# Two query-latent blocks as a column pair, closer last attention steps, alternating output blocks, and a fourth seven-product quad in the last pair

## The chip, the cores and the metric

The kernel runs on one core of a Trainium2 chip. Five engines share the work: TensorE (PE, matrix products and transposes), VectorE (DVE), ScalarE (ACT), GpSimd (POOL) and SyncE (SP, which only issues DMAs here). The metric is the time of one execution on the device in microseconds (us).

## The reference

The reference is a two-layer decoder trunk on x of 256 rows by 2048 columns, all in fp32. Layer 0 is retention with 8 heads and an MLP; layer 1 is multi-head latent attention with 16 heads and an MLP. Cut to the parts that the change touches:

```python
def mla_attention(h, w_dq, q_norm, w_uq, ...):        # layer 1
    c_q = rms_norm(h @ w_dq, q_norm)                  # 2048 -> 1536, the query latent
    q = (c_q @ w_uq).reshape(b, s, H, 128 + 64)       # 16 heads
    ...                                               # norms, rope, causal softmax over k_nope, k_pe
    return o @ w_o                                    # 2048 -> 2048

def sq_relu_mlp(h, w1, w2):                           # 2048 -> 8192 -> 2048
    return jnp.square(jax.nn.relu(h @ w1)) @ w2

x = x + mla_attention(rms_norm(x, norm_mix[1]), ...)
x = x + sq_relu_mlp(rms_norm(x, norm_mlp[1]), w1, w2)
```

## The kernel before, in words

**Products in fp32.** TensorE gets every fp32 operand as a high and a low part. ACT makes the high part by a cast (L185, or L188 with a scale), VectorE the low part by subtracting it from the source (L186, or L189). One product is then three matmuls: high by high, high by low, low by high. Activations (`act_tile`, 24 buffers) hold both parts of two 128-wide slices of the contraction for all 256 rows.

**Weights** come in chunks of up to 1 MB on SP's queue into `raw` (4 buffers) and are split half by half into tiles `wh` and `wl` of 128 x 1024 (5 buffers each). TensorE reads them in the same order, so a low-part tile that VectorE makes late holds TensorE up, and VectorE can be ahead by no more than five tiles.

**Plain products.** `gemm` computes a block of 512 columns (or fewer) over all chunks: 24 matmuls for one chunk of 512 columns.

**Column pairs.** `gemm_pair` (L335) computes two blocks of 512 columns together. Each chunk (a `quad`, L282) is a 2 x 2 block product: two row tiles of 128 by two slices of the contraction, times two slices by two column blocks. It takes either eight products (24 matmuls) or, after Strassen and Winograd, seven (21 matmuls). A seven needs sums of the weights, made by three VectorE additions (L321, L324, L325), four low-part tiles in place of two, and sums of the activations, which `with_sums` (L392 to L400) makes on VectorE with one more split. The tuples `THREE`, `FOUR` and `HEAD` list which quads of eight are sevens. `pair_out` (L367) copies six accumulators out of PSUM on ACT and finishes the combination with four VectorE additions; then every block is the sum of two parts, which are added later into x or by `summed` (L389).

**The order of the work.** Python code walks through the weight chunks. `later(n, fn)` puts a step n chunks ahead, `tick` runs the steps that have come due after each chunk, and `need` runs steps early until a wanted activation exists. A scheduler then fixes each engine's order of instructions at build time; on the chip every engine executes in that order.

**PSUM.** Four banks `acc` hold accumulators. Two banks `tp` take turns for transposes, attention outputs and two of the pair's products. A two-bank tile `at` holds the scores or the pair's last two products.

**Layer 1.** `into_next` adds the last MLP result into x, transposes and splits it twice, for the kv projection (`act_kv`) and for the query latent (`act_q`). The kv projection `kd` has two blocks; `downed` (L860) evacuates them and queues the transposes `kpe_tp` and `ckvtp` two chunks later. The query latent `dq` is three `gemm` blocks of four chunks (L934), each evacuated by `queried` (L912). Eight chunks `ku` make keys and values. Then `uq` makes the queries of two heads at a time, b = 0 to 7, three chunks each; `query` (L978) queues a turn three chunks later that transposes (`qntp`, `qptp`), that queues `score` (L1018) three later, that queues the transposes `ptp` three later, and those `values` (L1068) two later, which leaves the attention output `ao` in a `tp` bank until ACT and VectorE have split it into `ot`. The output projection `wo` (`gemm_blocks`, L418) starts with blocks 0 and 1, three chunks of block 0 and then three of block 1, and then the last chunk of each, which needs the last heads. The MLP of layer 1 has four groups of hidden columns; the last group ends with the pair `d_30` (columns 0 to 1023, eight quads), called the last pair here, and the plain blocks `d_32` and `d_33`. `finish` (L1086) adds each block into x and writes it out.

Of the kernel before, what the change touches and what calls it, by code (L numbers as in the profile page):

```python
# [15 lines left out]
AF = mybir.ActivationFunctionType  # L16
ALU = mybir.AluOpType
# [3 lines left out]
P = 128  # L21
NT = 2
# [18 lines left out]
S = NT * P  # L41
D = 2048
KD = D // P
NB = 4
# [2 lines left out]
NOPE, ROPE, MV, KVR, QR = 128, 64, 128, 512, 1536  # L47
KV_NBS, Q_NB = (320, 256), 384
GROUPS = (4, 4, 4, 4)
THREE, FOUR, HEAD = (3, 5, 7), (1, 3, 5, 7), (2, 4, 6, 7)  # L50
PI = math.pi

G_MIX0, G_MLP0, G_KV, G_MIX1, G_MLP1 = 0, 16, 32, 48, 64
# [15 lines left out]
def yoco(ctx: ExitStack, tc: tile.TileContext, a):  # L69
# [29 lines left out]
    def later(n, fn):  # L99
        queue.append((clock[0] + n, next(count), fn))  # L100
# [317 lines left out]
    def gemm_blocks(w, chunk_of, act, nk, name, done):  # L418

        n = nk // 4  # L420
        first = [accs(512, f"{name}{b}") for b in range(2)]
        for b in range(2):
            for g in range(n - 1):
                piece(w, chunk_of(b) + g, first[b], act, g, nk, 512, f"{name}{b}")
        for b in range(2):
            last_piece(w, chunk_of(b), first[b], act, nk, 512, f"{name}{b}", lambda acc, b=b: done(b, acc))
        for b in range(2, NB):
            gemm(w, chunk_of(b), act, nk, 512, f"{name}{b}", lambda acc, b=b: done(b, acc))

    def x_block_t(blocks, b, g0s, outs, name, sums):  # L430

        for k2 in range(2):
            tp = transposed(
                lambda t, j: blocks[t][:, (2 * k2 + j) * P : (2 * k2 + j + 1) * P], f"{name}_tp{b}{k2}"
            )
            for g0, out in zip(g0s, outs):
                scales = [gain(g0 + b * 4 + k2 * 2 + j) for j in range(2)]
                v = act_tile(f"{name}{g0}_{b}{k2}")
                if not sums:
                    split_act(v, tp, scales)  # L440
                    out.append(v)
                elif 2 * b + k2 in FOUR:
                    u = f2k([2, S], f"{name}u_{b}{k2}")
                    for j in range(2):
                        nc.scalar.activation(u[:, j], tp[:, j], AF.Copy, scale=scales[j])
                    split_act(v, u)
                    out.append((v, with_sums(u, f"{name}{b}{k2}")))
                else:
                    split_act(v, tp, scales)
                    out.append((v, None))  # L450
# [13 lines left out]
            if ss is not None:  # L464
                square_sum(x[t][b], ss[t][:, b : b + 1], f"{name}_{t}{b}")

    def into_next(ss, g0s, outs, r, name, sums=False):


        def done(b, acc):  # L470
            add_to_x(acc, b, ss, name)
            blocks = [x[t][b] for t in range(NT)]
            for t in range(NT):
                nc.gpsimd.dma_start(x_home[t][b], blocks[t])
            later(1, lambda: x_block_t(blocks, b, g0s, outs, name, sums))
            if b == NB - 1:
                r.extend(x_rstd(ss, name))

        return done
# [223 lines left out]

    ss = [small(NB, f"ss1_{t}") for t in range(NT)]
    act, r = [], []
    into_n1 = into_next(ss, [G_MLP0], [act], r, "n1", True)
    halves = [[], []]

    def ret_projected(h, qk, gate, v, s):
# [74 lines left out]
    def mlp(layer, act, r, done):  # L784
        w1, w2 = a[f"mlp_w1_{layer}"], a[f"mlp_w2_{layer}"]
        f0 = 0
        for gi, nf in enumerate(GROUPS):
            hid, blocks = [], []
            last = gi == len(GROUPS) - 1

            def up(c, p, hid=hid, blocks=blocks, last=last):

                need(r, NT)
                c = summed(c)
                for t in range(NT):
                    for i in range(2):
                        nc.scalar.activation(c[t][i], c[t][i], AF.Relu, scale=r[t])

                def turn(i):
                    for q in (2 * i, 2 * i + 1):  # L800
                        name = f"hid{layer}_{p}{q}"
                        tp = transposed(
                            lambda t, j: c[t][q // 2][:, (q % 2 * 2 + j) * P : (q % 2 * 2 + j + 1) * P], f"{name}_tp"
                        )
                        u = f2k([2, S], f"{name}_u")
                        nc.scalar.activation(u, tp, AF.Square)
                        v = act_tile(name)
                        split_act(v, u)
                        blocks.append((v, with_sums(u, name) if len(blocks) in (THREE if last else FOUR) else None))
                        hid.append(v)  # L810

                later(0, lambda: turn(0))
                later(1, lambda: turn(1))

            for p in range(f0 // 2, (f0 + nf) // 2):
                kinds = THREE[not (p or layer) :] if p % 2 or not p else FOUR
                gemm_pair(
                    w1, p * 8, act, [i in kinds for i in range(8)], f"u{layer}_{p}", lambda c, p=p, up=up: up(c, p)
                )
            if last:  # L820
                x_tiles(f"mlp{layer}")
            for p in range(2):
                if last and p and layer:
                    for b in (2, 3):
                        need(hid, 2 * nf)
                        gemm(
                            a["mlp_w2t"], (b - 2) * nf, hid, 4 * nf, 512, f"d{layer}_{gi}{b}",
                            lambda acc, b=b: done(b, acc),
                        )
                    continue  # L830

                def add(c, p=p, last=last):
                    into_x(done, c, p) if last else to_home(c, p)

                kinds = [i in (FOUR if p and not last else THREE) for i in range(2 * nf)]
                gemm_pair(w2, p * 32 + 2 * f0, blocks, kinds, f"d{layer}_{gi}{p}", add)
            f0 += nf

    ss = [small(NB, f"ss2_{t}") for t in range(NT)]
    act_kv, act_q, r2 = [], [], []  # L840
    mlp(0, act, r, into_next(ss, [G_KV, G_MIX1], [act_kv, act_q], r2, "n2"))


    def pe_rope(dst, u, src, t, i, heads):
# [15 lines left out]
    def downed(acc, b):  # L860
# [33 lines left out]
                split_act(v, tp, [gain(G_CKV + 2 * k2 + j) for j in range(2)])  # L894
                ckv.append(v)

        later(2, turn)

    first = [accs(n, f"kd{b}") for b, n in enumerate(KV_NBS)]
    for rows in (range(2), range(2, 4)):  # L900
# [8 lines left out]
    ssq = [small(3, f"ssq{t}") for t in range(NT)]  # L909
    cq, rq = [], []  # L910

    def queried(acc, b):  # L912
        cqb = []
        for t in range(NT):
            c = f2k([512], f"cq{b}{t}")
            nc.scalar.activation(c, acc[t], AF.Copy, scale=r2[t])
            square_sum(c, ssq[t][:, b : b + 1], f"cq{b}{t}")
            cqb.append(c)
            if b == 2:
                tot = small(1, f"cqtot{t}")  # L920
                nc.vector.reduce_sum(tot, ssq[t], axis=AX.X)
                rq.append(rstd(tot, QR, 1, f"cq{t}"))

        def turn():
            for k2 in range(2):
                tp = transposed(lambda t, j: cqb[t][:, (2 * k2 + j) * P : (2 * k2 + j + 1) * P], f"cqtp{b}{k2}")
                v = act_tile(f"cq{b}{k2}")
                split_act(v, tp, [gain(G_CQ + b * 4 + 2 * k2 + j) for j in range(2)])
                cq.append(v)

        later(1, turn)

    for b in range(3):
        gemm(a["mla_w_dq"], b * 4, act_q, KD, 512, f"dq{b}", lambda acc, b=b: queried(acc, b))  # L934


    k_t, v_s, vs = [], [], []
# [38 lines left out]
    def query(acc, b):  # L976
# [28 lines left out]
        def turn():  # L1005
            tp = transposed(lambda t, j: qr[t][0][:, j, 0:NOPE], f"qntp{b}")
            raw = f2k([2, S], f"qt{b}")
            nc.scalar.activation(raw, tp, AF.Copy, scale=gqn)
            qt = [f2k([2, S], f"qt{b}{i}", F32R) for i in range(2)]
            split(qt[0], qt[1], raw)  # L1010
            tp = transposed(lambda t, j: qr[t][1][:, j].rearrange("p i c -> p (i c)"), f"qptp{b}")
            qpe = f2k([2, S], f"qpe{b}", F32R)
            nc.scalar.copy(qpe, tp)
            later(3, lambda: score(b, qt, qpe))

        later(3, turn)

    def score(b, qt, qpe):  # L1018

# [36 lines left out]
        def turn():  # L1056
            pt = []
            for hh in range(2):
# [3 lines left out]
                o = f2k([3 * P], f"pt{b}{hh}")  # L1062
                nc.scalar.copy(o, tp)
                pt.append(o)
            later(2, lambda: values(b, pt))

        later(3, turn)

    def values(b, pt):
        o = bank("tp", [2, S], f"ao{b}")  # L1070
        for hh in range(2):
            nc.tensor.matmul(o[:, hh], v_s[b][:, 0, hh], pt[hh][:, 0:S], start=True, stop=False)
            nc.tensor.matmul(o[:, hh, P:S], v_s[b][:, 1, hh], pt[hh][:, S:], start=False, stop=True)
        v = act_tile(f"ot{b}")
        split_act(v, o)
        o_act.append(v)

    for b in range(8):
# [2 lines left out]
    ss = [small(NB, f"ss3_{t}") for t in range(NT)]  # L1081
    act, r = [], []
    x_tiles("wo")
    gemm_blocks(a["mla_w_o"], lambda b: b * 4, o_act, KD, "wo", into_next(ss, [G_MLP1], [act], r, "n3", True))

    def finish(b, acc):  # L1086
        add_to_x(acc, b, None, "")
        for t in range(NT):
            nc.sync.dma_start(a["out"][t * P : (t + 1) * P, b * 512 : (b + 1) * 512], x[t][b])

    mlp(1, act, r, finish)
    while queue:
# [93 lines left out]
```

## Time and profile before

| what | value |
|---|---|
| median of 3 runs | 2477.12 us (2475.17 to 2477.81) |
| profiled execution | 2474.51 us |
| its span | 2472.7 us |
| granted TensorE clock | 1.00 |
| ACT busy in the span | 1606.1 us (65%) |
| HBM read | 479.14 MB |

The span runs from the first to the last instruction of the program; the execution's time holds 1.8 us around it. A row of the waits gives the waiting engine, line and tile, the engine, tile and line that it waited for, and then the sum in us, how often, and the longest. A row of the windows gives length, and for each engine the busy time and the number of instructions. A row of the timeline gives start and length in us from the start of the span, engine, line, operation, output and inputs. A tile's name ends with a stage or block: `d_wl` is a low-part tile of an MLP's second matrix, `dq_wl` one of the query latent.

### The profile page before, as it was taken

What the parts mean: (1) busy time and instruction counts of PE and PEld (TensorE: products, weight loads), DVE (VectorE), ACT (ScalarE), POOL (GpSimd) and SP (SyncE); (2) the same over time, 40 slices, a digit from 0 to 9 for tenths busy, and PEclk for the clock granted to TensorE, in tenths of its full rate; (3) what the DMA queues carried; (4) which work ended last, traced back from release to release, by engine and by line L of the source; (5) the groups of instructions that cost most, each with busy time, mean ns of one, the idle gap of its engine ahead of it and who ended that gap; (6) DMA issues with size and microseconds to landing.
All of it is one profiled execution on the core that took longest, in us unless ns stands there. A gap on an engine that the chain in (4) does not pass through costs nothing.

```text
span 2472.7 us, 31711 instructions
## 1 busy us (share of the span) xinstructions
PE 2455.6 (99%) x11635; PEld 2060.0 (83%) x11635; DVE 2167.4 (88%) x2805; ACT 1606.1 (65%) x2253; POOL 251.6 (10%) x310
## 2 busy tenths in 40 slices
PE   9999999999999999999999999999999999999999
PEld 7888888888888888888888888998888888888887
DVE  7799899889899999999999967776689999999996
ACT  6566656556676667667666766676566666676663
POOL 7300011000010010110110101110000201101100
PEclk9999999999999999999999999999999999999999
DMA  9555567555564685684785564445545856857854
GB/s 328 211 174 205 196 205 234 199 192 201 198 236 182 209 262 216 213 254 172 246 263 196 192 228 168 153 155 179 199 174 199 261 212 209 268 203 225 266 192 153
DMA packets 93403, 521.04 MB, mean 211 GB/s; under 512 B 11072, under 2 KB 12224, under 8 KB 40000
## 3 DMA queue, kind: packets, MB, share of 16 engines
q1 hardware_dynamic: 71856, 472.83, 53.8%
q0 software_dynamic: 21248, 46.15, 8.5%
q8 instruction: 91, 1.49, 0.2%
q14 instruction: 64, 0.52, 0.1%
q10 hardware_dynamic: 144, 0.05, 0.0%
HBM read 479.14 MB, written 39.85 MB: 210 GB/s over the span
## 4 chain that ended last, share of the span: by engine, by line
PE 91%; DVE 4%; ACT 3%; issue 1%; POOL 1%; DMA 0%; SPq 0%; ACTq 0%; POOLq 0%; DVEq 0%
PE u_c L358 7%; PE u_c L356 7%; PE u_c L357 7%; PE d_c L357 6%; PE d_c L358 6%; PE d_c L356 6%; PE rk_acc L274 2%; PE rq_acc L274 2%; PE rp_c L356 2%; PE rp_c L357 2%; PE rp_c L358 2%; PE u_p L358 2%; PE u_p L356 2%; PE u_p L357 2%; PE d_p L356 2%; PE d_p L358 2%
## 5 line engine op out<-in xcount | busy, mean ns | idle before, releaser
L185 ACT CAST u_wh<-u_raw 128x1024 fp32r<-128x1024 f32 x362 | 347.9, 991 | 207.8 <-DVE u_raw L321 100.8
L185 ACT CAST d_wh<-d_raw 128x1024 fp32r<-128x1024 f32 x358 | 344.1, 993 | 202.5 <-DVE d_raw L321 93.9
L186 DVE TENSOR_TENSOR u_wl<-u_raw,u_wh 128x1024 fp32r<-128x1024 f32 x362 | 402.0, 1144 | 47.2 <-ACT u_wh L185 41.7
L186 DVE TENSOR_TENSOR d_wl<-d_raw,d_wh 128x1024 fp32r<-128x1024 f32 x358 | 397.8, 1146 | 40.1 <-ACT d_wh L185 35.5
L356 PE MATMUL u_c<-u_wh,n 128*128 128x512 f32 x706 | 276.4, 392 | 0.0
L357 PE MATMUL u_c<-u_wl,n 128*128 128x512 f32 x706 | 275.5, 390 | 0.0
L358 PE MATMUL u_c<-u_wh,n 128*128 128x512 f32 x706 | 274.9, 389 | 0.0
L356 PE MATMUL d_c<-d_wh,hid 128*128 128x512 f32 x654 | 256.0, 392 | 0.0
L357 PE MATMUL d_c<-d_wl,hid 128*128 128x512 f32 x654 | 255.4, 391 | 0.0
L358 PE MATMUL d_c<-d_wh,hid 128*128 128x512 f32 x654 | 254.6, 389 | 0.0
L185 ACT CAST rp_wh<-rp_raw 128x1024 fp32r<-128x1024 f32 (+1 forms) x166 | 160.7, 982 | 140.9 <-DVE rp_raw L321 64.9
L186 DVE TENSOR_TENSOR rp_wl<-rp_raw,rp_wh 128x1024 fp32r<-128x1024 f32 (+1 forms) x166 | 184.9, 1137 | 26.7 <-ACT rp_wh L185 24.4
L358 PEld LDWEIGHTS u_c<-u_wh,n 128*128 128x128 f32 x706 | 132.6, 188 | 27.4
L356 PEld LDWEIGHTS u_c<-u_wh,n 128*128 128x128 f32 x706 | 132.6, 188 | 26.9
L357 PEld LDWEIGHTS u_c<-u_wl,n 128*128 128x128 f32 x706 | 132.6, 188 | 26.7
L358 PEld LDWEIGHTS d_c<-d_wh,hid 128*128 128x128 f32 x654 | 122.8, 188 | 25.4
L356 PEld LDWEIGHTS d_c<-d_wh,hid 128*128 128x128 f32 x654 | 122.8, 188 | 25.2
L357 PEld LDWEIGHTS d_c<-d_wl,hid 128*128 128x128 f32 x654 | 122.9, 188 | 24.7
L150 POOL DMA_DIRECT2D xh<-d_c x48 | 41.6, 867 | 856.6 <-ACT d_c L373 854.7
L185 ACT CAST ro_wh<-ro_raw 128x1024 fp32r<-128x1024 f32 x88 | 85.7, 997 | 59.7 <-DVE ro_raw L321 25.7
L356 PE MATMUL rp_c<-rp_wh,a 128*128 128x512 f32 x286 | 111.9, 391 | 0.0
L357 PE MATMUL rp_c<-rp_wl,a 128*128 128x512 f32 x286 | 111.4, 390 | 0.2 <-DVE rp_wl L186 0.2
(465 smaller groups left out, 6075.6 us busy)
## 6 DMA issues: line engine op xcount, KB each, us to landing
u_raw<-in_mlp_w SPq DMA_DIRECT2D x128, 1024.0 KB, 5.2
d_raw<-in_mlp_w SPq DMA_DIRECT2D x120, 1024.0 KB, 4.9
rp_raw<-in_ret_w_gv SPq DMA_DIRECT2D x56, 1024.0 KB, 4.9
ro_raw<-in_ret_w_out SPq DMA_DIRECT2D x32, 1024.0 KB, 4.9
uq_raw<-in_mla_w_uq SPq DMA_DIRECT2D x24, 768.0 KB, 4.1
rq_raw<-in_ret_w_qk SPq DMA_DIRECT2D x16, 1024.0 KB, 5.0
rk_raw<-in_ret_w_qk SPq DMA_DIRECT2D x16, 1024.0 KB, 4.8
wo_raw<-in_mla_w_o SPq DMA_DIRECT2D x16, 1024.0 KB, 4.8
```

The costliest lines, as they stand in the source:

```text
L150: nc.gpsimd.dma_start(x_home[t][2 * p + j], part, accum_op=ALU.add)
L185: nc.scalar.copy(h, src)
L186: nc.vector.tensor_tensor(l, src, h.bitcast(F32), op=ALU.subtract)
L274: nc.tensor.matmul(acc[f], wh[:, cols], a.rearrange("p i s -> p (i s)"), start=k == 0, stop=k == nk - 1)
L356: nc.tensor.matmul(dst, ah, bh, start=n == 0, stop=False)
L357: nc.tensor.matmul(dst, ah, bl, start=False, stop=False)
L358: nc.tensor.matmul(dst, al, bh, start=False, stop=n == total[key] - 1)
```

## The change

1. The first two of the three dq blocks become a `gemm_pair` whose quads 4 to 7 are sevens (`QUERY`); the third stays a `gemm`. The activations of those four quads are copied scaled to SBUF by ACT, and their sums are made by steps that wait 8 or 9 chunks (`sum_up`). The weights are laid out for it on the host.
2. The turn of `downed` waits three chunks in place of two.
3. In attention the steps of the last heads follow each other at fewer chunks, and `values` first copies `ao` to an SBUF tile `ou` on ACT and splits that.
4. `gemm_blocks` takes the chunks of blocks 0 and 1 of wo in turns.
5. In layer 1 the last pair has the sevens 2, 4, 6 and 7 (`HEAD`) where it had 3, 5 and 7 (`THREE`), and the sums of the activations follow.
6. `finish` issues each row tile's output DMA right after its additions, and cuts the last one in two halves.

```diff
-THREE, FOUR, HEAD = (3, 5, 7), (1, 3, 5, 7), (2, 4, 6, 7)
+THREE, FOUR, HEAD, QUERY = (3, 5, 7), (1, 3, 5, 7), (2, 4, 6, 7), (4, 5, 6, 7)
@@ gemm_blocks
-        for b in range(2):
-            for g in range(n - 1):
+        for g in range(n - 1):
+            for b in range(2):
                 piece(w, chunk_of(b) + g, first[b], act, g, nk, 512, f"{name}{b}")
@@ x_block_t
-                elif 2 * b + k2 in FOUR:
+                elif 2 * b + k2 in sums:
                     u = f2k([2, S], f"{name}u_{b}{k2}")
                     for j in range(2):
                         nc.scalar.activation(u[:, j], tp[:, j], AF.Copy, scale=scales[j])
                     split_act(v, u)
-                    out.append((v, with_sums(u, f"{name}{b}{k2}")))
+                    if wait is None:
+                        out.append((v, with_sums(u, f"{name}{g0}_{b}{k2}")))
+                        continue
+                    out.append([v, None])
+
+                    def sum_up(u=u, pair=out[-1], name=f"{name}{g0}_{b}{k2}"):
+                        pair[1] = with_sums(u, name)
+
+                    later(wait + k2, sum_up)
@@ mlp
-                        blocks.append((v, with_sums(u, name) if len(blocks) in (THREE if last else FOUR) else None))
+                        blocks.append((v, with_sums(u, name) if len(blocks) in ((HEAD if layer else THREE) if last else FOUR) else None))
...
-                kinds = [i in (FOUR if p and not last else THREE) for i in range(2 * nf)]
+                kinds = [i in ((HEAD if layer else THREE) if last else FOUR if p else THREE) for i in range(2 * nf)]
...
-    mlp(0, act, r, into_next(ss, [G_KV, G_MIX1], [act_kv, act_q], r2, "n2"))
+    mlp(0, act, r, into_next(ss, [G_KV, G_MIX1], [act_kv, act_q], r2, "n2", [(), QUERY], 8))
@@ downed
-        later(2, turn)
+        later(3, turn)
@@ queried
-        later(1, turn)
-
-    for b in range(3):
-        gemm(a["mla_w_dq"], b * 4, act_q, KD, 512, f"dq{b}", lambda acc, b=b: queried(acc, b))
+        later(wait, turn)
+
+    def queried_pair(c):
+        c = summed(c)
+        for j in range(2):
+            block = [c[t][j] for t in range(NT)]
+            queried(block, j, 1 + j, block)
+
+    gemm_pair(a["mla_w_dq"], 0, act_q, [k in QUERY for k in range(8)], "dq0", queried_pair)
+    gemm(a["mla_w_dq2"], 0, [v for v, _ in act_q], KD, 512, "dq2", lambda acc: queried(acc, 2, 1))
@@ query
-            later(3, lambda: score(b, qt, qpe))
+            later((3, 2, 1)[max(b - 5, 0)], lambda: score(b, qt, qpe))
-        later(3, turn)
+        later(3 if b < 7 else 2, turn)
@@ score
-            later(2, lambda: values(b, pt))
+            later(2 if b < 6 else 1, lambda: values(b, pt))
-        later(3, turn)
+        later(3 if b < 5 else 2, turn)
@@ values
+        u = f2k([2, S], f"ou{b}")
+        nc.scalar.copy(u, o)
         v = act_tile(f"ot{b}")
-        split_act(v, o)
+        split_act(v, u)
@@ finish
-        add_to_x(acc, b, None, "")
-        for t in range(NT):
-            nc.sync.dma_start(a["out"][t * P : (t + 1) * P, b * 512 : (b + 1) * 512], x[t][b])
+        for t in range(NT):
+            cuts = 2 if b == NB - 1 and t == NT - 1 else 1
+            n = 512 // cuts
+            for i in range(cuts):
+                for part in acc[t] if isinstance(acc[t], tuple) else (acc[t],):
+                    y = x[t][b][:, i * n : (i + 1) * n]
+                    nc.vector.tensor_tensor(y, part[:, i * n : (i + 1) * n], y, op=ALU.add)
+                nc.sync.dma_start(a["out"][t * P : (t + 1) * P, b * 512 + i * n : b * 512 + (i + 1) * n], y)
```

## The prediction

> **What bounds the kernel now.** I read the page's busy times and slices first, then the chain that ended last:
>
> ```profile
> PE 2455.6 (99%) x11635; PEld 2060.0 (83%) x11635; DVE 2167.4 (88%) x2805; ACT 1606.1 (65%) x2253; POOL 251.6 (10%) x310
> DVE  7799899889899999999999967776689999999996
> PE 91%; DVE 4%; ACT 3%; issue 1%; POOL 1%; DMA 0%; SPq 0%; ACTq 0%; POOLq 0%; DVEq 0%
> ```
>
> TensorE is the bound by its share, but VectorE is at nine tenths in most slices, and the slices that are not (24 to 31, attention and around it) are where half of this change lies. Next the waits of TensorE:
>
> ```profile
> PE qptp L205 <- DVE ot L186: 1.9, 1, 1.9
> PE qptp L205 <- ACT qt L1008: 1.2, 1, 1.2
> PE kpe_tp L205 <- ACT kpp L883: 0.8, 1, 0.8
> PE kpe_tp L205 <- DVE kpp L884: 0.4, 1, 0.4
> PE wo_acc L246 <- ACT ot L185: 0.3, 1, 0.3
> ```
>
> These five are all that the change could remove as waits, 4.6 us. Then the busy times by stage: the end of the kv projection, the query latent (dq), attention with the start of wo, and the last pair with what follows it:
>
> ```profile
> core 0: us, PE busy (x) PEld busy (x) DVE busy (x) ACT busy (x) POOL busy (x), PEclk, DMA share, GB/s
> 1405.00:1436.00 31.00, 30.95 (x227) 29.84 (x226) 27.80 (x53) 26.45 (x60) 4.27 (x8) 1.00 0.70 246
> 1436.00:1500.00 64.00, 62.77 (x291) 51.82 (x290) 36.36 (x52) 36.42 (x63) 5.64 (x8) 1.00 0.58 198
> 1590.00:1700.00 110.00, 106.84 (x674) 102.97 (x673) 83.18 (x211) 79.28 (x169) 17.48 (x14) 1.00 0.49 167
> 2380.00:2430.00 50.00, 50.00 (x229) 41.28 (x228) 49.04 (x62) 36.55 (x49) 0.00 (x0) 1.00 0.57 207
> 2430.00:2460.00 30.00, 30.00 (x134) 24.82 (x134) 17.95 (x19) 10.55 (x10) 0.00 (x0) 1.00 0.40 141
> ```
>
> The reader is to see that dq leaves VectorE 28 of 64 us free, and the last pair leaves it 1 of 50. The granted clock is 1.00 in all of them. Last, the timeline of the two engines in the last pair (start, length, instruction):
>
> ```profile
> 2383.18 0.69 DVE L375 TENSOR_TENSOR u_v<-u_p,u_p 128x512 f32<-128x512 f32 x1
> 2405.88 1.22 DVE L321 TENSOR_TENSOR d_raw<-d_raw 128x1024 f32<-128x1024 f32 x1
> 2407.13 0.69 DVE L324 TENSOR_TENSOR d_raw<-d_raw 128x512 f32<-128x512 f32 x1
> 2407.86 0.69 DVE L325 TENSOR_TENSOR d_raw<-d_raw 128x512 f32<-128x512 f32 x1
> 2408.47 6.86 DVE L186 TENSOR_TENSOR d_wl<-d_raw,d_wh 128x1024 fp32r<-128x1024 f32 x6
> 2420.26 0.69 DVE L463 TENSOR_TENSOR x_mlp<-d_c,x_mlp 128x512 f32<-128x512 f32 x1
> 2440.04 0.39 PE L248 MATMUL d_acc<-d_wh,hid 128*128 128x512 f32 x1
> 2440.26 0.39 PE L246 MATMUL d_acc<-d_wh,hid 128*128 128x512 f32 x1
> ```
>
> A matmul of 512 columns lasts 0.39 but the next starts 0.227 later; that pitch is the price of one. On VectorE independent instructions start 1.14 apart (1024 columns), 0.60 (512), 0.34 (256) and 0.20 (128); the three additions of a seven-product quad depend on each other and take 2408.47 - 2405.88 = 2.59.
>
> **Part by part.** *Prices of a quad.* Eight products: 24 matmuls, 5.44 us of TensorE, two subtractions, 2.28 of VectorE. Seven products: 21 matmuls, 4.77 us, and 3 x 1.14 + 0.60 + 2.59 = 6.6 on VectorE. A seven saves 0.68 of TensorE and costs VectorE 4.3, and it needs sums of the activations: 0.34 + 0.20 + 0.20 + 0.60 = 1.35. So a lone seven is paid from VectorE's lead, and the lead is bounded by five low-part buffers, four of which one seven fills.
>
> *dq.* Four sevens instead of eights in the pair: 12 matmuls less, -2.7. They are quads 4, 5, 6 and 7, in a row. The first tile of quad 5 waits for the buffer of quad 3's last tile, so VectorE begins it about 1.05 (one cast) after quad 4 starts; from there to the last tile are three sevens, 19.2 to 19.9, and some four matmuls (0.9) follow: the pair ends 21.2 to 21.9 after quad 4's start, where TensorE alone needs 4 x 4.77 = 19.1. Stall 2.2 to 2.8; I take 2.5. Two sevens in a row show almost none: in retention's pairs TensorE waits 0.2 to 0.7 at a time for the subtraction. The four sums (5.4 us of VectorE) come due with the first quads, where VectorE has 28 us free; that cover hides them. The pair's copies and additions (ACT six, VectorE eight) lie beside block 2's 24 x 4 matmuls; the same handover happens at every pair of the MLPs, where matmul starts between 640 and 1340 us lose 1.7 us in all.
>
> *kv projection.* Four copies of 512 columns more on ACT (2.1 us) in a stretch where it has 4.5 of 31 us free, and the pair needs all four accumulators at its start where dq's first block needed two: the second two are emptied by 1436.4, its third product starts 1435.02 + 6 x 0.227 = 1436.4. Between nothing and 1.5; I take 0.5.
>
> *kpe_tp a tick later.* Its two stalls (starts of the transposes late by 0.98 and 0.58) go: -1.6. Behind it ckv is later by one quad and still eight chunks ahead of its first use.
>
> *Attention.* Start-to-start the transposes lose 2.04 at head 2 (qptp), 0.27 at head 6, 1.34 at head 7 and 0.51 before wo. At head 2 the bank is now released by an ACT copy instead of cast and subtraction:
>
> ```profile
> 1625.90 0.57 ACT L185 CAST ot<-ao 128x512 fp32r<-128x512 f32 x1
> 1626.90 0.68 DVE L186 TENSOR_TENSOR ot<-ao,ot 128x512 fp32r<-128x512 f32 x1
> 1627.64 0.66 PE L205 MATMUL qptp<-cst,qpp 128*128 128x128 f32 x4 [1.88 <-DVE ot L186]
> ```
>
> The copy ends at 1626.4 instead of 1627.6: -1.2. The 0.27 goes. The last heads' closer steps take away most of 1.34 + 0.51, but ptp then waits on qpe's copy and ao on the second pt copy, 1.1 us together: -0.75. Sum -2.2, bounds -1.0 and -3.3. Eight more copies (0.5 each) on ACT have cover: it is busy 79 of 110 us. Alternating wo's blocks moves the need for heads 5 and 6 back by one or two chunks (5.4 us each) and costs no instruction. The POOL queue's loads of x keep their number and lie tens of us before use.
> The Trainium skill (VectorE: DVE Perf Modes, Rules for kernel authors) advises copying out of PSUM first only if many operations follow. Here two follow, and the subtraction takes 686 ns from PSUM and 694 (hid) from SBUF, so the copy buys VectorE nothing; by that rule it would only lengthen head 7's way into wo by 0.5, and the sum would be 0.5 higher.
>
> *Last pair.* One seven more: -0.7. VectorE ran from 2383.18 to 2420.26 without a gap, and quad 7 used its last low tile 2.9 us after that was done. Now the same queue holds 4.3 (the seven) + 1.35 (one more set of sums) + 1.2 (two of the x additions, which the order puts ahead of the last tile) = 6.9 more: the last tile is ready at 2427.1. Quad 7, 0.7 earlier, wants it at its 17th matmul, 2419.2 + 3.6 = 2422.8; products of high parts alone can run ahead for 0.7. Stall 3.6 to 4.3. Then the next block (d_32) waits 0.3 for its first tile, and its third tile stands behind that block's first two tiles and eight additions of the pair (8 x 0.60), ready at 2427.1 + 2 x 1.14 + 4.8 + 1.14 = 2435.4 against 2433.8: 1.6. I take 5.5; bounds 2.5 (the additions give way, part of the lead survives) and 6.5. VectorE is 40% idle from 2430, so nothing is passed on further.
>
> *Tail.* The last addition of 512 columns is cut in two, the last DMA halved: -0.2. The weight loads that stand behind finish's output DMAs on SP are needed 15 us later: nothing.
>
> *Sum.* -2.7 + 2.5 + 0.5 - 1.6 - 2.2 - 0.7 + 5.5 - 0.2 = +1.1 us, on a profiled execution of 2474.51 (span 2472.7). That execution is 2.6 us below the median of the three runs, 2477.12, so on the scale of the median: 2478.2. Some 0.2% (5 us) is what a measurement here can tell from no change.
>
> **Rivals.** *Faster: TensorE alone decides.* If VectorE's lead covers the sevens, both stalls (8.0) go and the sum is -6.9: 2470.2. For it: TensorE is busy 99%, and the sevens already there stall it by tenths. Against it: those come singly or in twos, and no row shows four. The Trainium skill (Perfetto Trace Analysis, Identifying the Most-Contended Engine) says to optimize the engine of highest occupancy first; by it these 15 matmuls pay in full. The trace agrees for the span and not for 2380 to 2430, where VectorE has 49.04 of 50 us.
>
> *Slower: the late sums of dq are too late.* If quad 4 starts before its four sums are made, TensorE waits for them at c12's product, and they push the queue of low parts back: up to 5.4 more, sum +6.5, 2483.6. It decides from the point where VectorE is less than one set (1.35) ahead at quad 4. For it: they stand behind ckv and kpe in the same queue, and VectorE executes in order. Against it: 28 us free.
>
> *The attention part does nothing*: ptp and ao wait on ACT as long as qptp did on VectorE. Sum +3.3, 2480.4; still within 0.2%, and counted with the forecast.
>
> **How the numbers follow.** Forecast (with the third rival) 0.45, faster rival 0.30, slower rival 0.25: VectorE's bound in the last pair is read from a gapless queue, the one in dq is argued. The range holds the forecast's bounds (+1.1 with -3.7 and +3.7 from the single bounds) and reaches the faster rival with its attention at -3.3 (2469) and the slower one (2484).
>
> **What would show it.** Right: TensorE waiting on d_wl subtractions for 3 to 5 us around 2420 and 1 to 2 near 2434, on dq_wl for 2 to 3 in quads 6 and 7, no wait of kpe_tp, qptp at head 2 under 1. Wrong: no such waits (faster rival); a wait of the first matmuls of dq's quad 4 on an activation's sums (slower rival); or new waits on ACT in attention's last heads over 2 us.

## The result and the profile after

The changed kernel takes 2487.18 us (median of 6 runs, 2485.4 to 2487.53) against 2475.12 for the kernel before (6 runs, the three of the table above among them). The ratio is 1.0044, with a 95% interval of 1.0031 to 1.0057: slower by 12 us, where +1.1 was forecast and the range ended at 2484. The profiled execution took 2487.53, its span 2485.7.

The busy times and the slices of VectorE in the page of the changed kernel:

```profile
PE 2460.7 (99%) x11620; PEld 2057.4 (83%) x11620; DVE 2200.3 (89%) x2855; ACT 1624.3 (65%) x2286; POOL 248.6 (10%) x310
...
DVE  7799899888899999999999988776689999999996
```

TensorE has 15 matmuls less, and VectorE's slices 24 and 25, where dq lies, have gone from 6 and 7 tenths to 8. The waits of TensorE:

```profile
...
PE dq_p L356 <- ACT dq_wh L185: 2.4, 3, 0.9
PE qptp L205 <- ACT ou L1090: 2.3, 4, 1.1
PE ptp L1076 <- ACT qt L1023: 1.6, 1, 1.6
PE dq_c L356 <- ACT dq_wh L185: 1.4, 2, 0.7
PE d_c L356 <- ACT d_wh L185: 1.4, 2, 0.7
PE d_acc L247 <- DVE d_wl L186: 1.4, 1, 1.4
...
PE dq_p L357 <- DVE dq_wl L186: 0.7, 2, 0.5
PE ptp L1076 <- ACT qpe L1028: 0.6, 1, 0.6
```

The two kpe_tp waits and the qptp wait on VectorE are gone, as forecast. In their place stand waits in dq (4.5 us), in attention (4.5) and in the last pair (2.8). The windows of the same stages:

```profile
1436.00:1500.00 64.00, 59.34 (x262) 46.16 (x261) 57.64 (x90) 45.87 (x83) 5.64 (x8) 1.00 0.52 181
...
1590.00:1700.00 110.00, 107.73 (x672) 103.79 (x671) 83.53 (x215) 78.83 (x164) 17.48 (x14) 1.00 0.49 163
1700.00:1740.00 40.00, 37.80 (x198) 31.65 (x197) 19.83 (x26) 27.11 (x58) 0.00 (x0) 0.96 0.41 135
...
2380.00:2430.00 50.00, 49.08 (x221) 39.07 (x220) 48.05 (x62) 33.62 (x46) 0.00 (x0) 1.00 0.50 174
```

VectorE was idle for 28 of the 64 us of dq before; now for 6. And between 1700 and 1740 the granted clock was 0.96.

For the rest of the document one table is enough. It compares the starts of the first matmul of each stage, of the last up-projection matmul (where the last pair begins) and of the last matmul in the trace of a run with those in the trace of before and gives by how many us each stretch became longer (+) or shorter. The stretches up to dq's start are left out: in the retention stage, the same code in all of these, single traces differ by -0.2 to +1.9 us. So are ku (within 0.02 of before) and the MLP up to its last up-projection (-0.1 to +0.4). All runs are in it; what each one is follows below.

| run | dq (to ku) | uq to wo | wo to the MLP | last pair to the last matmul | tail |
|---|---|---|---|---|---|
| changed kernel | +3.05 | +0.68 | +2.93* | +4.42 | +0.52 |
| dq_alone | +3.00 | +1.88* | +0.01 | +0.01 | +0.01 |
| dq_57 | -0.97 | +1.55* | +0.01 | -0.02 | +0.01 |
| dq_early | +1.76* (kv projection +8.08*) | +1.57* | +0.01 | +0.01 | +0.02 |
| kpe_fin | -1.33 | +1.57* | +0.01 | +0.01 | +0.53 |
| kpe_uncut | -1.33 | +1.55* | +0.01 | +0.01 | 0.00 |
| att_alone | +0.01 | +0.46 | +2.34* | +0.01 | 0.00 |
| ou_alone | +0.03 | +0.41 | +4.81* | +0.01 | +0.03 |
| steps_alt | 0.00 | -0.01 | -0.99 | +0.01 | +0.03 |
| alt_alone | +0.01 | +1.57* | +0.39 | +0.01 | +0.02 |
| pair_alone | +0.01 | 0.00 | 0.00 | +4.41 | 0.00 |
| pair_nosums | +0.01 | +0.01 | +0.01 | +0.56 | +0.02 |
| after_no_ou | +3.04* | +1.85* | -1.00 | +4.41 | +0.54 |
| best1 | -2.32 | +0.47 | +0.01 | +0.01 | +0.01 |
| best2 | -2.32 | +1.55* | -0.97 | +0.01 | 0.00 |
| best3 | -2.32 | +0.49 | -0.97 | -0.02 | +0.03 |

A star marks a stretch in whose trace the granted clock fell behind waits of TensorE; its mean over 20 us there is 0.83 to 0.91. In the changed kernel's trace this fell on the stretch from wo to the MLP:

```profile
1700.00:1705.00 5.00, 4.09 (x33) 3.68 (x31) 2.92 (x4) 5.00 (x12) 0.00 (x0) 1.00 0.61 210
1705.00:1710.00 5.00, 3.70 (x13) 3.10 (x14) 3.97 (x7) 4.21 (x13) 0.00 (x0) 0.69 0.63 210
1710.00:1715.00 5.00, 5.00 (x24) 4.10 (x24) 1.58 (x3) 3.71 (x9) 0.00 (x0) 0.97 0.00 0
```

The last columns are the granted clock, the share of the DMA engines and GB/s: 5 x 0.31 + 5 x 0.03 = 1.7 us of that stretch's +2.93 is the clock. dq_early has two such stretches, from 1438.3 to 1441.7 in the kv projection and from 1445.1 to 1448.5 in dq; what they cost there is not told apart from the waits that follow them.

### The profile page after: what moved, and what is told of

Its sections match the earlier page's. It is cut to its first block, busy times and chain, and to the rows that moved or that the text cites. A ratio compares the mean times of both kernels' runs of the same rounds, so it can differ in the third digit from the quotient of the medians.

```text
span 2485.7 us, 31776 instructions
## 1 busy us (share of the span) xinstructions
PE 2460.7 (99%) x11620; PEld 2057.4 (83%) x11620; DVE 2200.3 (89%) x2855; ACT 1624.3 (65%) x2286; POOL 248.6 (10%) x310
## 4 chain that ended last, share of the span: by engine, by line
PE 86%; DVE 7%; ACT 4%; issue 1%; POOL 1%; DMA 0%; SPq 0%; ACTq 0%; DVEq 0%; POOLq 0%
PE u_c L358 7%; PE u_c L357 7%; PE u_c L356 7%; PE d_c L357 6%; PE d_c L358 6%; PE d_c L356 6%; PE rk_acc L274 2%; PE rq_acc L274 2%; PE rp_c L356 2%; PE rp_c L357 2%; PE rp_c L358 2%; PE u_p L358 2%; PE u_p L357 2%; PE u_p L356 2%; PE d_p L356 2%; PE d_p L357 2%
## 5 line engine op out<-in xcount | busy, mean ns | idle before, releaser
L356 PE MATMUL d_c<-d_wh,hid 128*128 128x512 f32 x648 | 253.0, 392 | 1.4 <-ACT d_wh L185 1.4
L358 PE MATMUL d_c<-d_wh,hid 128*128 128x512 f32 x648 | 252.4, 389 | 0.0
```

What stands on the lines that cost most here:

```text
L356: nc.tensor.matmul(dst, ah, bh, start=n == 0, stop=False)
L358: nc.tensor.matmul(dst, al, bh, start=False, stop=n == total[key] - 1)
```

## The experiments

### Each part alone

Theory A was that each part costs by itself what the trace of the changed kernel shows in its stage; rival B that the parts cost little alone and their combination costs. In the first run only the change to the query latent was made (part 1 as in the diff above), in the second only the last pair, in the third attention (parts 3 and 4), in the fourth kpe_tp and the output step.

```diff
 dq_alone:   part 1 only (kpe_tp two chunks later, as before)
 pair_alone: +kinds = [i in ((HEAD if layer else THREE) if last else FOUR if p else THREE) ...]   and its sums
 att_alone:  +later((3, 2, 1)[max(b - 5, 0)], score) ... +nc.scalar.copy(u, o) ... +for g ...: for b in range(2)
 kpe_fin:    +later(3, turn) in downed, +the new finish
```

> The kernel before with part 1 alone (query latent as a column pair with sevens 4 to 7, sums late). Theory A (each part costs by itself what the trace of the changed kernel shows in its stage): TensorE loses about 6 us in quads 4 to 7 and keeps its two kpe_tp stalls; less 2.7 us of matmuls, so +3 to +4 us against before. Rival B (the parts cost little alone, their combination costs): within 1 us of before.

> The kernel before with the sevens 2, 4, 6 and 7 in the last pair alone, the output step as before. Theory A: TensorE waits about 5 us more between quad 4 and the third tile of the next block, less 0.7, so +4 to +5 us. Rival B: the x additions that the new output step puts ahead of the last low part are the cause; without them under +2 us.

> The kernel before with parts 3 and 4 alone (closer last steps, copy of ao, alternating blocks of wo). Theory A: the stall before ptp at the last heads (2.5 us in the changed kernel) and the lower clock behind it come by themselves: +2 to +4 us. Rival B: they come from the shift that dq brings; alone the part gains the 2 us that were forecast.

> The kernel before with the later kpe_tp (part 2) and the new output step (part 6) alone. Theory A: the two kpe_tp stalls go (-1.6 us) and the end of the kernel is within 0.5 us of before: -1 to -2 us. Rival B: the kpe_tp stalls only move to the next transposes, and the output step costs: 0 to +1 us.

Measured, with the ratio to before: dq_alone 2481.26 (1.0017, interval 1.0008 to 1.0027), pair_alone 2479.65 (1.0014, 1.0004 to 1.0024), att_alone 2478.14 (1.0007, 0.9997 to 1.0016), kpe_fin 2475.75 (0.9995, 0.9986 to 1.0004); before 2476.17 in the same session. The differences of the medians are +5.1, +3.5, +2.0 and -0.4, together +10.1 of 12. They hold the clock as well: all ten runs of dq_alone have a mean granted clock of 0.999 or 0.998, seven of the ten of pair_alone 1.0. The table says more: each part alone shows in its own stage what it shows in the whole, 3.00 against 3.05, 4.41 against 4.42, and the tail 0.53 against 0.52. Rival B falls for dq, the last pair and attention, and with it the idea that the x additions of the new output step delay the last pair. For kpe_fin neither expectation holds whole: it gains 0.8 us by the table where A had 1 to 2 and B none, and the output step costs, as B had it. Nor does dq_alone lose the 6 us in quads 4 to 7 that A named, but 4.1. Only kpe_tp does not add up: alone it gains 1.33 in dq, but dq_alone, which keeps the kpe_tp stall, and the whole, which does not, both come out at +3.0.

### Query latent: pace, or late sums

VectorE in the changed kernel's quads 4 to 7, from its timeline:

```profile
1460.86 0.68 DVE L325 TENSOR_TENSOR dq_raw<-dq_raw 128x512 f32<-128x512 f32 x1
1461.46 0.29 DVE L397 TENSOR_TENSOR n_sum<-n_sum,n2u 128x128 f32<-128x128 f32 x1
1461.78 0.29 DVE L398 TENSOR_TENSOR n_sum<-n2u,n_sum 128x128 f32<-128x128 f32 x1
1462.72 1.23 DVE L186 TENSOR_TENSOR dq_wl<-dq_raw,dq_wh 128x1024 fp32r<-128x1024 f32 x1 [0.64 <-ACT dq_wh L185]
1463.86 0.69 DVE L186 TENSOR_TENSOR n_more<-n_sum,n_more 128x512 fp32r<-128x512 f32 x1
1464.46 1.82 DVE L186 TENSOR_TENSOR dq_wl<-dq_raw,dq_wh 128x1024 fp32r<-128x1024 f32 x2
1466.20 1.22 DVE L321 TENSOR_TENSOR dq_raw<-dq_raw 128x1024 f32<-128x1024 f32 x1
...
1472.94 1.22 DVE L321 TENSOR_TENSOR dq_raw<-dq_raw 128x1024 f32<-128x1024 f32 x1
...
1479.68 1.22 DVE L321 TENSOR_TENSOR dq_raw<-dq_raw 128x1024 f32<-128x1024 f32 x1
```

From 1466.20 on one seven takes VectorE 6.74 us, twice the same, without a gap; TensorE needs 4.77. The waits are put down to ACT's cast (`dq_wh`) only because the cast of the last two tiles comes behind VectorE's additions. And in front of it, at 1461 to 1464, the last set of sums stands among quad 4's low parts: VectorE has no lead when the row begins. Two runs were to separate pace and late sums.

```diff
 dq_57:    -QUERY = (4, 5, 6, 7)   +QUERY = (5, 7)
 dq_early: -into_next(..., "n2", [(), QUERY], 8)   +into_next(..., "n2", [(), QUERY])
```

> Part 1 alone with two sevens that stand apart, quads 5 and 7, in place of four in a row. Theory A (VectorE needs 6.7 us for a seven against 4.8 of TensorE, so sevens in a row run at VectorE's pace; one between eights is paid from its lead): no wait of TensorE in quads 4 to 7 over 0.5 us, six matmuls less (-1.4 us), and the start of ku 1 to 2 us earlier than with four in a row made it, from -1.4 to 0 against before. Rival B (the late sums and the kv latent in VectorE's queue are the cause, whatever the spacing): waits of 2 us or more remain, ku starts later than before.

> Part 1 alone, sevens 4 to 7, but each set of sums is made at once with its activation, in the kv projection, and not late. Theory A (pace of four sevens in a row): the waits in quads 5 to 7 stay at 1.5 to 1.9 us each, 4 us or more in all. Rival B (the late sums stand in front of the low parts of quad 4 and 5): the waits fall to the 2.5 us of the forecast, and the kv projection pays up to 5 us in its place.

With sevens 5 and 7, TensorE waits nowhere in quads 4 to 7 by more than 0.2 us, and ku starts 0.97 earlier: 2475.5 against 2475.76 (ratio 0.9999, 0.9990 to 1.0009), its profile with the lower clock of the star. Theory A holds for two sevens that stand apart; but with two sevens there are also only two late sums, so this run does not tell the row from the sums. With early sums four in a row still wait, in the last two quads:

```profile
PE kd_acc L246 <- ACT n L188: 2.7, 2, 2.4
PE dq_c L356 <- ACT down L872: 2.2, 1, 2.2
...
PE dq_p L356 <- ACT dq_wh L185: 1.4, 2, 0.9
...
PE dq_c L356 <- ACT dq_wh L185: 0.7, 1, 0.7
```

By the starts of the matmuls quads 6 and 7 lose 0.63 + 0.89 + 1.10 + 0.70 = 3.3 us, against 5.9 in quads 4 to 7 of the changed kernel and 4.1 in dq_alone. Neither expectation is met whole: the pace alone costs 3.3, more than the 2.5 of the forecast and less than the 4 of theory A. In the changed kernel quads 6 and 7 lose 3.5, nearly the same, and quads 4 and 5 the other 2.4. These 2.4 are put down to the late sums, which stand among the low parts there; that is not shown alone, since TensorE comes to dq_early's quads some 8 us later and so leaves VectorE more time. Moving the sums does not help: the kv projection pays 8.1 us (2486.06 in all, ratio 1.0039, 1.0024 to 1.0055). It also accounts for kpe_tp. Where VectorE sets the end of dq, TensorE that no longer waits at kpe_tp arrives earlier and waits longer at the sevens: 2.2 us of kpe_tp and 4.1 in the quads in dq_alone, 0 and 5.9 in the whole.

### Last pair: volume, or the chain in each seven

pair_alone has the waits of the changed kernel to the digit:

```profile
PE d_c L356 <- ACT d_wh L185: 1.4, 2, 0.7
PE d_acc L247 <- DVE d_wl L186: 1.4, 1, 1.4
```

They name the cast, so a chain additions, cast, subtraction would explain them as well as a full queue. The next run leaves out VectorE's sums, and with each set one cast on ACT, and changes nothing of that chain.

```diff
-blocks.append((v, with_sums(u, name) if ...))
+blocks.append((v, (v if layer and last else with_sums(u, name)) if ...))
```

> The kernel before with the sevens 2, 4, 6 and 7 in the last pair, and no sums of the activations in that last group: the four VectorE operations and the cast of each set are left out and the activations themselves stand in their place, so what the sevens multiply is not the right operand. Theory A (the volume of VectorE's queue sets the last pair's end): 5.4 us less in the queue, so the waits of 3.8 us in quads 3 to 7 and the next block fall under 1 us and the kernel is 0.5 to 1 us faster than before. Rival B (the chain inside each seven, additions then cast then subtraction, makes the waits on ACT's casts): the waits stay at 3 us or more.

The d_c waits are gone and one of 0.4 is left; the stretch is +0.56 in place of +4.41:

```profile
PE d_acc L247 <- DVE d_wl L186: 0.4, 1, 0.4
```

Theory A holds: 5.4 us of VectorE less takes 3.85 us off the end. The four casts that go with the sums are not a likely cause, since ACT was busy for 33.6 of the 50 us, but no run takes them away alone. One point of the expectation was not met: even then the fourth seven does not gain its 0.68, and the kernel was to be 0.5 to 1 us faster than before. In all 2476.94 against 2475.76 (ratio 1.0004, 0.9994 to 1.0015).

### Attention: the closer steps, or the copy

In the changed kernel the wait of 1.6 us before ptp looks like the work of the closer steps. ACT and TensorE around it:

```profile
1703.10 1.97 ACT L185 CAST wo_wh<-wo_raw 128x1024 fp32r<-128x1024 f32 x2
1704.98 0.68 ACT L1023 ACTIVATE qt<-qntp,gqn 128x512 f32<-128x512 f32 x1
```

```profile
1703.69 0.40 PE L1048 MATMUL s<-kpe_t,qpe 128*128 128x256 f32 x2
1705.71 0.55 PE L1076 MATMUL ptp<-cst,p 128*128 128x128 f32 x3 [1.62 <-ACT qt L1023]
```

ptp wants the bank of qntp, and the ACT copy that frees it is queued behind two casts of weights. My theory A was that the closer steps make this; rival B blamed the copy of ao.

```diff
 ou_alone:  +nc.scalar.copy(u, o), split_act(v, u)        steps and wo as before
 steps_alt: closer steps and alternating blocks            no copy
 alt_alone: alternating blocks only
```

> The kernel before with the copy of every ao to SBUF alone. Theory A (the bank is freed by one ACT copy, but ACT's queue now decides every handover): the stall of qptp near 1627 falls from 2.0 to about 0.9 us, and new ones of 0.4 to 0.8 appear at the three pairs of heads after it; from start of uq to start of wo +0.3 to +0.7 us, the rest unchanged. Rival B (the copy gains what was forecast): -1 us or better, no new stall.

> The kernel before with the closer last steps and the alternating blocks, without the copy of ao. Theory A (the closer steps put transposes, score and softmax of two pairs of heads into one stretch of ACT's queue, whatever the copy): the stall before ptp, 1.8 + 0.6 us, and the lower clock behind it stay; from start of wo to the MLP +2 to +3 us. Rival B (the copy is the cause): under 0.5 us there.

> The kernel before with the alternating blocks of wo alone, steps as before. Theory A: the order of wo's chunks by itself moves nothing, or takes up to 0.5 us of the stall before wo away: from start of wo to the MLP -0.5 to 0. Rival B (alternating is what moves the last heads together): +1 us or more there.

For steps_alt theory A is wrong. Without the copy the closer steps gain 0.99 us, the wait before ptp is 0.5 (`PE ptp L1061 <- ACT qpe L1013: 0.5, 1, 0.5`), and no lower clock follows in its trace: 2474.82 against 2476.3 (ratio 0.9996, 0.9986 to 1.0006). The copy alone loses, in more than the way theory A had it: the first qptp behind an ao falls from 2.04 to 0.93 as forecast, 0.43, 0.44 and 0.81 appear at the next ones, and the last one loses 3.06 where it had lost 1.34. 2478.41 (ratio 1.0009, 0.9999 to 1.0019). ACT and TensorE of ou_alone at that place:

```profile
1698.93 1.97 ACT L185 CAST wo_wh<-wo_raw 128x1024 fp32r<-128x1024 f32 x2
1700.81 0.57 ACT L1075 COPY ou<-ao 128x512 f32<-128x512 f32 x1
```

```profile
1701.43 1.12 PE L205 MATMUL qptp<-cst,qpp 128*128 128x128 f32 x4 [2.87 <-ACT ou L1075]
```

ao was finished at 1698.1, its copy came at 1700.81, behind the casts. The alternating blocks alone move the end of attention by +0.39 (2476.03, ratio 0.9999, 0.9989 to 1.0009): wo then waits 1.3 us for the last `ot` in place of 0.3; neither expectation was met. The closer steps without the alternating blocks were not run. Whether the same holds inside the whole was tried by undoing the copy alone.

```diff
-u = f2k([2, S], f"ou{b}"); nc.scalar.copy(u, o); split_act(v, u)
+split_act(v, o)
```

> The changed kernel with one thing undone, the copy of ao to SBUF. Theory A (the copy makes the loss of attention in the whole kernel as it does alone): from start of uq to the MLP it is 3 to 5 us faster than the changed kernel, with at most 0.7 us of waiting before ptp, and about 2483 us in all. Rival B (with dq's shift the closer steps lose by themselves): the stretch stays within 1 us of the changed kernel's.

It does: 2484.44, which is 8.4 us above before in its session where the changed kernel was 12.1 above; from wo to the MLP -1.00 where the whole had +2.93, and a wait of 0.5 before ptp. From uq to the MLP the gain is 2.8 us in this trace, a little under what was expected. Both traces have one stretch of lower clock there, of 1.7 us, this one behind qptp and the changed kernel's behind ptp, so the clock cancels in the 2.8.

### The tail

In kpe_fin the time from the last matmul to the end is 0.53 longer. The next run keeps the order of additions and DMAs and undoes the cut.

```diff
-cuts = 2 if b == NB - 1 and t == NT - 1 else 1
+cuts = 1
```

> As the run of the later kpe_tp and the output step, but the last addition and its DMA are not cut in two. Theory A (the second half-size DMA and the third issue cost at the end): the time from the last matmul to the end goes back from 5.3 to about 4.8 us. Rival B (the order of adding and issuing costs): it stays at 5.3.

The tail is back at 0.00: theory A. 2475.15 (ratio 0.9995, 0.9986 to 1.0004). The cut costs half a microsecond more than the shorter addition saves. The half-size transfers land no sooner (2.6 us after their issue, where the whole ones take 2.5), and the third issue starts 0.2 us later behind the last matmul than the second did; what makes up the rest is not shown.

### What is left standing, put together

best1 takes dq_57, the later kpe_tp, and the copy of ao for the first pair of heads alone. best2 takes dq_57, kpe_tp, the closer steps and the alternating blocks. best3 is best2 and that one copy.

```diff
+        if b == 0:                      # best1, best3
+            u = f2k([2, S], f"ou{b}")
+            nc.scalar.copy(u, o)
+            o = u
         split_act(v, o)
```

> A version put together from what the runs left standing: query latent as a pair with the sevens 5 and 7 only, the later kpe_tp, and the copy of ao for the first pair of heads alone; last pair, last steps, wo and output as before. Theory A: -2.7 us by the start of ku (kpe_tp stalls and six matmuls), -1.1 at the first qptp behind an ao, and fewer lower-clock stretches behind that stall: 3 to 5 us faster than before. Rival B: without the kpe_tp stall TensorE arrives at the sevens earlier and waits there, as with four in a row: -1.5 us or less.

> The changed kernel with four things undone: sevens 5 and 7 in dq in place of 4 to 7, no copy of ao, the last pair and the output as before. Theory A (the parts add up): -2.3 us by the start of ku, -1.0 from start of wo to the MLP, so 3 to 4 us faster than before, apart from lower-clock stretches. Rival B (the last steps gain only with the copy or with dq's shift): -2.5 us or less.

> The second combined version and the copy of ao for the first pair of heads alone. Theory A (one copy frees the bank where the 2 us stall stands, keeps the clock up behind it, and the other heads keep their order): no stretch at a lower clock near 1630 in the profile, start of uq to start of wo +0.5, start of wo to the MLP -1.0, about 2472 us and 4 us faster than before. Rival B (one copy upsets the closer steps as eight did): +1 us or more from start of wo to the MLP, 2473.5 us or more.

| run | median us | before us | ratio (interval) |
|---|---|---|---|
| best1 | 2472.91 | 2476.3 | 0.9987 (0.9978 to 0.9996) |
| best2 | 2473.05 | 2476.03 | 0.9987 (0.9978 to 0.9996) |
| best3 | 2472.28 | 2476.23 | 0.9985 (0.9976 to 0.9994) |

All three beat both kernels, best3 by 4.0 us against before. The parts add up in the table to a tenth of a microsecond: -2.32 in dq, +0.47 to +0.49 for one copy, -0.97 for the steps. One copy moves the stall (2.04 becomes 0.94 there and 1.57 at the next qptp in best1), so by the table it loses 0.5. What it brings is the clock: the mean granted clock is 1.0 in all 11 runs of best1 and 0.999 in 7 of best2's 11. The four runs of best2 at 1.0 have a median of 2472.1, as good as best3, so the copy buys no more than the clock. With one copy the closer steps keep their 0.97, so it is the other seven copies that lose in the whole. The timelines put most of it on the last heads, behind the casts of wo; those copies were not run alone.

## Why the prediction was wrong, point by point

- *dq: -2.7 + 2.5 for the row of sevens, with four late sums hidden by 28 us of free VectorE.* This step failed. The pace of a seven was right (6.6 forecast, 6.74 measured), the stall was not: 5.9, of which 3.3 is pace and the rest, as far as the runs tell, the late sums. The free time lies before the last low parts of quad 4 are made, not around them: sums, kv latent and low parts of the first sevens meet between 1450 and 1464. The slower rival had half of this mechanism: the sums push the low parts back, by up to 5.4 us. It came with 0.3 in quad 4 and 2.1 in quad 5; for the sums themselves TensorE never waited. I counted a stage's mean idle time as cover for work that comes due in a quarter of it.
- *kpe_tp: -1.6.* Right alone (-1.33), nothing in the whole. I added two terms that share one slack: where the row of sevens ends when VectorE ends, a stall taken from TensorE ahead of it is handed on.
- *kv projection: +0.5.* It costs nothing (+0.03); ACT's copies and the four accumulators fit.
- *Attention: -2.2.* This step failed, and it was the largest miss: +3.6. The closer steps, with the alternating blocks, gained about what was foreseen for the last heads (-0.75 forecast, -0.99 measured). The copy of ao was costed from the one place where it helps (-1.2 forecast, -1.1 measured) and hidden elsewhere because ACT is busy 79 of 110 us. But it put ACT's queue between each ao and the next transpose, and at wo's start that queue holds two casts of 0.95 each. The prediction's own sign for it, new waits on ACT of over 2 us in the last heads, came: 1.6 and 0.6 before ptp. (The 694 ns that it gives the subtraction of hid are 690 in the profile; nothing hangs on it.) The sentence on the Trainium skill's rule, by which such a copy does not pay for two readers (VectorE: DVE Perf Modes, Rules for kernel authors), pointed the right way, though with 0.5 us and not with this mechanism.
- *Last pair: -0.7 + 5.5.* Right in cause and size, not in place: the table's +4.42 with its -0.68 makes a stall of 5.1. The queue reached quad 7's last tile, counted from the same instruction (2391.22), after 43.3 us (end of the first of the three at 2433.36, 1.14 long) where 43.9 was worked out, and TensorE's wait for the third tile of the next block was 1.5 (1.6 forecast). pair_nosums shows that it is the volume. But the 3.6 to 4.3 that were put on quad 7 alone came as 0.7 in quad 2, 1.4 in quad 4 and 1.2 in quad 7, by the starts of the matmuls.
- *Tail: -0.2.* It was +0.52; the cut costs, where it was put at a gain.
- *Clock: not in the forecast.* The stall that the closer steps and the copy make together brought 1.7 us of lower clock, counted in the +3.6.

The misses make 4.4 (dq with kpe_tp and kv projection: -1.3 forecast, +3.05 measured), 5.8 (attention) and 0.7 (tail), less 0.4 in the last pair: 10.5 us on a forecast of 1.1, which is 11.6, close to the 12.1 of the medians.

The faster rival (VectorE's lead covers the sevens) is refuted in both places: TensorE at 99% lost 15 matmuls and the kernel got slower. The prediction read the Trainium skill's rule on the engine of highest occupancy (Perfetto Trace Analysis, Identifying the Most-Contended Engine) without its exception: for TensorE the rule takes not the busy share of the matmuls but, beside the share of the peak rate, that of the weight loads. By that share TensorE has 83% in the profile of before and VectorE 88%, so the rule read whole points to VectorE, and the runs agree with it.

## What to carry to other kernels

A stage's idle time on an engine is cover only where it lies: work that comes due in a burst is to be added up against that burst, and two savings that end at the same bound are one saving. A product that saves the busiest engine 0.7 us and costs the next one 4.3 is paid from the lead between the two, so such products pay only where the next engine has time between them: two apart gained in dq, four in a row lost there, and so did a fourth in the last pair, where VectorE was already full. And a copy that frees a bank early does so only when it reaches the head of its engine's queue: look at what is queued in front of it at each place, not at the engine's share.

## What the runs showed of the hardware

Behind some waits of TensorE the granted clock falls for a while, in some executions and not in others. The same stall of qptp (2.04 us near 1628) is followed by a mean clock of 1.00 in the window of 20 us in steps_alt and 0.91 in alt_alone:

```profile
1620.00:1640.00 20.00, 18.13 (x117) 17.70 (x117) 15.91 (x41) 12.76 (x30) 2.31 (x1) 1.00 0.40 131
```

```profile
1620.00:1640.00 20.00, 18.13 (x108) 17.69 (x107) 15.91 (x41) 12.81 (x29) 2.31 (x1) 0.91 0.40 131
```

In windows of 1 us alt_alone shows what that mean hides, a clock of one half for about 3.4 us:

```profile
1630.00:1631.00 1.00, 1.00 (x9) 1.00 (x8) 0.96 (x5) 1.00 (x3) 0.06 (x1) 0.65 0.67 111
1631.00:1632.00 1.00, 1.00 (x6) 1.00 (x6) 0.75 (x1) 0.31 (x1) 1.00 (x1) 0.50 0.96 375
1632.00:1633.00 1.00, 1.00 (x6) 1.00 (x5) 0.00 (x0) 0.00 (x0) 1.00 (x1) 0.50 0.79 317
1633.00:1634.00 1.00, 1.00 (x6) 1.00 (x5) 0.72 (x3) 0.00 (x0) 0.25 (x1) 0.64 0.00 0
```

The shares that are missing, 0.35 + 0.50 + 0.50 + 0.36, make 1.7 us; the table's starred +1.55 to +1.57 is what it costs there. The other starred stretches have the same 1.7 us, and ou_alone's, behind a wait of 3.06, twice that. Where TensorE waits for VectorE anyway it costs nothing: after_no_ou has such a stretch in dq, from 1469.6 on, and its dq is +3.04 against +3.05 without one. It is in the times too: the runs of before at mean clock 1.0, 0.999 and 0.998 in the session of best1 have medians of 2475.45 (12 runs), 2476.45 (17) and 2478.18 (4).

The Trainium skill (TensorE: Matmul & The Clock Gate, What's actually happening) describes a clock gate that looks at activity in windows of 3.4 us which run freely, not from the kernel's start; that would make it vary between executions as it does here. It asks for an idle window of 3.4 us; here waits of 2 us amid transposes were enough, and so were two of 0.9 us within 1.5 us in after_no_ou's dq. Those of 0.94 and 1.57 in best1, 19 us apart, were not in its trace, and all its 11 runs have a mean clock of 1.0.
